# A gated-DeltaNet layer with memory attention: the memory's key products in another PSUM bank, their weights' splits listed 400 instructions earlier

## The chip, the cores and the metric

The kernel runs on one core of a Trainium2 chip. The metric is the device time of one execution in microseconds, as the median of several runs. A profiled execution gives the trace: a record of nearly every instruction on TensorE (PE, with its weight loads as PEld), VectorE (DVE), ScalarE (ACT), GpSimd (POOL) and SyncE (SP), and of the DMA transfers.

## The reference

One decoder layer over 2048 tokens of width 1024: eight heads of a gated delta rule (chunks of 64, head size 128) and four heads of cross-attention to a memory of 256 rows share one input projection and one output projection; then comes a squared-ReLU MLP, with a layer norm after each of the two.

```python
def gdn_mixer(x, mem_k, mem_v, w_in, ...):
    proj = x @ w_in                      # q, k, v, z of 8 heads, gates a, b, and mq of 4 memory heads
    qkv = silu(causal_depthwise_conv(qkv, conv_w))
    ...
    o = chunk_gated_delta_rule(l2_normalize(q), l2_normalize(k), v, g, beta)   # a state per head, chunk after chunk
    ...
def memory_attention(mq, mem_k, mem_v):
    s = einsum('bthd,bmhd->bhtm', q, mem_k) * MEM_HEAD_DIM ** -0.5
    p = softmax(s)
    return einsum('bhtm,bmhd->bthd', p, mem_v)
def sqrelu_mlp(x, w1, w2):
    return square(relu(x @ w1)) @ w2
```

The memory is normalised, and `mem_k` and `mem_v` are its products with `w_mem_k` and `w_mem_v`. They depend on no token, so the kernel makes them once, in its first block. `mem_k` is what the change is about: for each of four memory heads a product of 128 x 1024 by 1024 x 256.

## The kernel before, in words

**Stages.** The 2048 tokens are four blocks of 512. Two super-steps each take two blocks through `mixer` and then run the output projection (`out_seven`, accumulators `ao`) and the MLP (`ff1`, `ff2`, accumulators `fA`, `fB`, `fC`, `f2A` and so on). In `mixer` the eight heads are pipelined: while `dense` and `gate` project head t, `gdn_a` builds the decay matrices of head t-1 and `invert` inverts them, and `gdn_b` carries the state of head t-2 through four chunks of 128. In block 0 the memory's work is spread over the same steps: `memory_rows` first (it makes `mT`, the transposed memory), `memory_keys` for heads 0 and 1 in the next step, for 2 and 3 in the one after it, and then `memory_values`.

**Precision.** A float32 matrix is split into a high part, which ACT casts, and a low part, which DVE makes by a subtraction. `mm3` multiplies with three matmuls: high by high, high by low, low by high. Weights arrive by SP's DMA in `wraw` (three buffers) and are split into `whl` (four buffers): one cast and one subtraction of 128x1024 for a column of weights.

**Names.** `aq`, `ak`, `av`, `az` are the projections of a head, 24 matmuls of 128x512 each; `cq`, `ck`, `cv`, `cz` are what follows from them on ACT and DVE (`cz<-th,az` is the last reader of `az`). `amk` is a key product of the memory, 24 matmuls of 128x256, and `mst` its split, which is stored to `mscr`. `Lq`, `Lc`, `Bc`, `Xc`, `Z32`, `ZT`, `pq`, `pp`, `inv`, `Y` belong to the inverse of a head: `Bc` and `Xc` are a chain of small DVE instructions, `pq` and `pp` the small matmuls after it. `pkq` are products of keys and queries, `ptk`, `ptq`, `ptv` transposes; `vb` is made of `ptv`, `jk` and `kd` of `ptk`, on ACT. The state recurrence of `gdn_b` runs, for each chunk, `pc<-state,ck` and `po<-state,qd` on PE, `R` on DVE, `pc<-R,Y` on PE, `vt` on ACT, `pc<-vt,kd` and `po<-vt,at` on PE, and `state` on DVE.

**PSUM.** Banks are given out by tag: `PBUFS = {"acc": 3, "ga0": 1, "ga1": 1, "pb": 2, "m": 1}`. The projections take `acc`; the memory attention (from the sixth step of the heads on) takes the single bank `m`, which the gates and half of the memory's transposes have had before it.

**Order.** Nothing is issued as the code is run. A recorder notes each instruction with its number and a priority (`o.prio = o.i + self.shift`), and `issue` then replays all of them from line 402, for which reason every row of the profile has the line L402. It is a planner: with modelled durations it picks for each engine, of the instructions whose inputs and buffers are there, the one of the smallest priority. Buffers of a tag are promised in the order in which their first users were noted. Each engine then executes what stands in its list strictly in that order, so a row that waits holds up all that stand behind it.

Of the kernel before, what the change touches and what calls it, by code (L numbers as in the profile page):

```python
# [418 lines left out]
def hybrid_layer(  # L419
# [43 lines left out]
    def slot(name, tag="s0", dt=F32, shape=(P, TB)):  # L463
        return rec.buf(sp, shape, dt, tag, BUFS[tag], name)
# [4 lines left out]
    def bank(name, tag):  # L469
        return rec.buf(ps, (P, TB), F32, tag, PBUFS[tag], name)  # L470
# [32 lines left out]
    rec = Recorder(nc, tc)  # L503
# [25 lines left out]
    def split(src, hi, lo, eng=None):  # L529
        nc.scalar.copy(out=hi, in_=src)  # L530
        (eng or nc.vector).tensor_tensor(out=lo, in0=src, in1=hi.bitcast(F32), op=ALU.subtract)
# [6 lines left out]
    def hilo(src, eng=None):  # L538
        t, hi, lo = pair()
        split(src, hi, lo, eng)  # L540
        return t, hi, lo

    def as_cols(hi, lo):
        hi, lo = hi.rearrange("p (k f) -> p k f", k=KT), lo.rearrange("p (k f) -> p k f", k=KT)
        return [hi[:, k].part(k) for k in range(KT)], [lo[:, k].part(100 + k) for k in range(KT)]

    def mm3(o, lh, ll, rh, rl, start, stop, **kw):
        nc.tensor.matmul(o, lh, rh, start=start, stop=False, **kw)
        nc.tensor.matmul(o, lh, rl, start=False, stop=False, **kw)
        nc.tensor.matmul(o, ll, rh, start=False, stop=stop, **kw)  # L550

    def load_cols(w, u, eng=None):

        rt = rec.buf(wp, (P, 1024), F32, "wraw", NR, "wraw")
        nc.sync.dma_start(out=rt, in_=w[u])
        return as_cols(*hilo(rt, eng)[1:])
# [87 lines left out]
    def memory(step):  # L644
        if step == 0:
            memory_rows()
        elif step < 3:
            for h in (0, 1) if step == 1 else (2, 3):
                memory_keys(h)
        elif step == 3:  # L650
            memory_values()
# [17 lines left out]
            mx.append(t)  # L669

    def memory_keys(h):
        w = load_cols(w_mem_k, h)
        a = bank("amk", "acc")
        for k in range(KT):
            mm3(a[:, :M], w[0][k], w[1][k], mx[k // 2][:, 0, k % 2], mx[k // 2][:, 1, k % 2], k == 0, k == KT - 1)
        st = slot("mst", "th", F32R)
        split(a[:, :M], st[:, :M], st[:, M:])
        nc.sync.dma_start(out=mscr[h, :, :2 * M], in_=st.bitcast(F32))
# [1150 lines left out]
```

## Time and profile before

| | |
|---|---|
| median of three runs | 2760.96 us (2760.94 to 2762.19) |
| the profiled execution's own time | 2760.71 us |
| its span in the trace | 2759.0 us |
| mean granted TensorE clock | 0.997 |
| PE busy | 2719.8 us, 99% of the span, 13589 matmuls |
| DVE, ACT, POOL busy | 2112.2, 1642.3, 403.7 us |

The 1.7 us between the span and the execution's time lie around the program. In a row of the timeline stand the start, the width and the engine, then what is written and what is read, the shapes, and the number of instructions that follow one another without a gap; in brackets, how long the engine had been idle before it and whose end it had waited for. In a row of the windows stand the stretch and its length, then the busy time of PE, PEld, DVE, ACT and POOL with the number of instructions of each, the granted clock, and the share and the rate of the DMA. Where rows overlap a little, an engine has taken up the next instruction before the last one had left it; the cost of one instruction in a row of many is then the distance between two starts.

### The profile page before, as it was taken

To read this page: it belongs to the slowest core of one execution; us is meant where nothing else is said; L and a number is where in the kernel's file an instruction comes from. 1 tells how busy PE (TensorE), PEld (TensorE's weight loads), DVE (VectorE), ACT (ScalarE), POOL (GpSimd) and SP (SyncE) were. 2 spreads that over 40 slices of the span, in tenths; PEclk is the share of its full clock that TensorE was granted. 3 is DMA by queue.
4 is the path that set the end of the run, shared out by engine and by line. 5 is a ranking of instruction groups with operands and counts; after the bars stand their busy time and mean duration, and the time that the engine had idled before them with its cause. 6 is when DMAs were issued, how large, how long until landed. Compare 5 with 4: busy or idle time off the path is not lost.

```text
span 2759.0 us, 42405 instructions
## 1 busy us (share of the span) xinstructions
PE 2719.8 (99%) x13589; PEld 2267.0 (82%) x13589; DVE 2112.2 (77%) x5652; ACT 1642.3 (60%) x4082; POOL 403.7 (15%) x1030
## 2 busy tenths in 40 slices
PE   9999999999999999999999999999999999999998
PEld 7888888887788888888888888888887788888887
DVE  7889889998777777665778887888978665657575
ACT  7678767676485556334446676677855655544342
POOL 3233223321000000000023321223201000000000
PEclk9999999999999999999999999999999999999999
DMA  8565558876788888766754344444578744477673
GB/s 327 207 234 205 215 182 288 290 258 228 269 284 302 280 285 297 268 211 205 265 209 149 138 155 174 169 147 159 206 251 280 249 145 152 163 252 243 205 239 116
DMA packets 208543, 613.99 MB, mean 223 GB/s; under 512 B 23072, under 2 KB 32192, under 8 KB 188352
## 3 DMA queue, kind: packets, MB, share of 16 engines
q1 hardware_dynamic: 207888, 611.23, 63.5%
q8 instruction: 107, 1.75, 0.2%
q14 instruction: 116, 0.95, 0.1%
q10 hardware_dynamic: 432, 0.05, 0.0%
HBM read 436.54 MB, written 174.65 MB: 222 GB/s over the span
## 4 chain that ended last, share of the span: by engine, by line
PE 88%; ACT 7%; DVE 4%; issue 1%; POOL 1%; DMA 0%; DVEq 0%; SPq 0%; POOLq 0%; ACTq 0%
PE f2A L402 13%; PE fA L402 12%; PE ao L402 8%; PE f2C L402 6%; PE fC L402 6%; PE az L402 5%; PE aq L402 5%; PE av L402 5%; PE ak L402 5%; PE f2B L402 3%; PE fB L402 3%; PE amq L402 3%; PE pc L402 3%; PE po L402 2%; PE pkq L402 1%
## 5 line engine op out<-in xcount | busy, mean ns | idle before, releaser
L402 DVE TENSOR_TENSOR whl<-wraw,whl 128x512 fp32r<-128x512 f32 (+2 forms) x294 | 257.2, 884 | 109.4 <-ACT whl L402 107.0
L402 ACT CAST whl<-wraw 128x512 fp32r<-128x512 f32 (+2 forms) x294 | 226.5, 780 | 158.0 <-PE fC L402 52.0
L402 PE MATMUL fA<-B,whl 128*128 128x512 f32 x1152 | 277.2, 389 | 1.8 <-ACT B L402 1.5
L402 ACT CAST X<-X 128x1024 fp32r<-128x1024 f32 x118 | 123.9, 1052 | 236.2 <-DMA X<-xsc 196.2
L402 PE MATMUL f2A<-whl,X 128*128 128x512 f32 x1152 | 262.1, 389 | 0.0
L402 PEld LDWEIGHTS fA<-B,whl 128*128 128x128 f32 x1152 | 216.1, 188 | 47.5 <-ACT B L402 1.9
L402 PEld LDWEIGHTS f2A<-whl,X 128*128 128x128 f32 x1152 | 216.2, 188 | 44.9
L402 DVE TENSOR_TENSOR X<-X,X 128x1024 fp32r<-128x1024 f32 x118 | 144.2, 1223 | 129.0 <-ACT X L402 128.8
L402 PE MATMUL aq<-T,whl 128*128 128x512 f32 x768 | 214.3, 408 | 10.0 <-ACT T L402 5.5
L402 PE MATMUL az<-T,whl 128*128 128x512 f32 x768 | 213.0, 406 | 0.0
L402 PE MATMUL ak<-T,whl 128*128 128x512 f32 x768 | 211.4, 406 | 0.0
L402 PE MATMUL av<-T,whl 128*128 128x512 f32 x768 | 210.4, 404 | 0.0
L402 PE MATMUL fC<-B,whl 128*128 128x512 f32 x768 | 185.4, 389 | 0.3 <-DVE B L402 0.3
L402 PE MATMUL f2C<-whl,X 128*128 128x512 f32 x768 | 174.7, 389 | 0.0
L402 PEld LDWEIGHTS fC<-B,whl 128*128 128x128 f32 x768 | 144.1, 188 | 30.7 <-DVE B L402 0.8
L402 PEld LDWEIGHTS f2C<-whl,X 128*128 128x128 f32 x768 | 144.1, 188 | 29.9
L402 PEld LDWEIGHTS aq<-T,whl 128*128 128x128 f32 x768 | 136.5, 191 | 32.7 <-ACT T L402 5.5
L402 POOL TENSOR_SCALAR ve<-mv 128x1 f32<-128x1 f32 x34 | 16.4, 483 | 962.0 <-DVE mv L402 961.5
L402 PEld LDWEIGHTS av<-T,whl 128*128 128x128 f32 x768 | 137.3, 189 | 22.7
L402 PEld LDWEIGHTS ak<-T,whl 128*128 128x128 f32 x768 | 136.4, 189 | 23.5
L402 PEld LDWEIGHTS az<-T,whl 128*128 128x128 f32 x768 | 135.9, 189 | 21.6
L402 PE MATMUL ao<-whl,X 128*128 128x512 f32 x528 | 140.1, 404 | 3.5 <-DVE whl L402 1.3
(287 smaller groups left out, 6300.8 us busy)
## 6 DMA issues: line engine op xcount, KB each, us to landing
whl<-wsc SPq DMA_DIRECT2D x108, 1024.0 KB, 4.8
wraw<-in_w_ff_dram SPq DMA_DIRECT2D x106, 512.0 KB, 4.5
X<-xsc SPq DMA_DIRECT2D x96, 512.0 KB, 3.9
wsc<-whl SPq DMA_DIRECT2D x36, 1024.0 KB, 5.2
whl<-tsc SPq DMA_DIRECT2D x64, 512.0 KB, 4.7
xsc<-hB SPq DMA_DIRECT2D x96, 256.0 KB, 3.4
xo<-cat SPq DMA_DIRECT2D x80, 256.0 KB, 3.9
wraw<-in_w_in_dram SPq DMA_DIRECT2D x35, 512.0 KB, 5.9
```

Source lines behind the costliest of these rows:

```text
L402: o.fn(*[res(a) for a in o.args], **{k: res(v) for k, v in o.kw.items()})
```

## The change

The weights of a key product are now noted with priorities 400 smaller (the DMA, the cast and the subtraction), and the product takes the bank `m` in place of one of the three `acc`.

```diff
     def memory_keys(h):
+        rec.shift = -400
         w = load_cols(w_mem_k, h)
-        a = bank("amk", "acc")
+        rec.shift = 0
+        a = bank("amk", "m")
         for k in range(KT):
             mm3(a[:, :M], w[0][k], w[1][k], mx[k // 2][:, 0, k % 2], mx[k // 2][:, 1, k % 2], k == 0, k == KT - 1)
```

Since the planner starts from other priorities and other banks, the lists of all engines change, from the first key product on until the output projection of the first super-step; from there on they are the same again, instruction by instruction. Three places matter here.

PE, second head of block 0, at the first two key products; a piece of the difference. `az` is the gate's projection of the first head and `aq` the query projection of the second; `T_...` are the tokens.

```order
 L402 MATMUL az<-T_221,whl 128x512
-L402 MATMUL amk<-mT,whl 128x256 x4
+L402 MATMUL amk<-mT,whl 128x256 x24
 L402 MATMUL aq<-T_160,whl 128x512
 L402 MATMUL aq<-T_165,whl 128x512
-L402 MATMUL amk<-mT,whl 128x256 x44
 L402 MATMUL aq<-T_160,whl 128x512 x2
 L402 MATMUL aq<-T_165,whl 128x512
...
 L402 MATMUL aq<-T_226,whl 128x512
 L402 MATMUL aq<-T_221,whl 128x512 x2
+L402 MATMUL amk<-mT,whl 128x256 x24
 L402 MATMUL aq<-T_226,whl 128x512
```

Before, two key products (4 and 44 matmuls) stand around the first two matmuls of `aq`. Now one stands whole ahead of `aq`, and the other behind its twentieth matmul.

DVE, the same place, with the buffers' numbers. Before, the low halves of the two key weights (`whl_995`, `whl_1029`) and of `aq`'s weight (`whl_1056`, made of `wraw_862`) stand in one group behind `cz`:

```order
L402 SCALAR_TENSOR_TENSOR cz_1101<-th_1080,az_999 128x512
L402 STREAM_SHUFFLE Bc_114<-Xc_106 128x32
L402 STREAM_SHUFFLE Bc_116<-Xc_108 128x12
L402 TENSOR_TENSOR whl_995<-wraw_757,whl_995 128x1024
L402 TENSOR_TENSOR Bc_114<-Bc_114,Lc_962 128x32
L402 TENSOR_TENSOR Bc_116<-Bc_116,Lc_1060 128x12
L402 TENSOR_TENSOR whl_1029<-wraw_818,whl_1029 128x1024
L402 TENSOR_TENSOR Xc_106<-Xc_106,Bc_114 128x32
L402 TENSOR_TENSOR Xc_108<-Xc_108,Bc_116 128x12
L402 TENSOR_TENSOR whl_1056<-wraw_862,whl_1056 128x1024
```

Now the key weights' low halves stand some 50 rows earlier, and `aq`'s, again made of `wraw_862`, stands between the steps of the convolutions:

```order
L402 SCALAR_TENSOR_TENSOR ck_1010<-raw_704,cw_96,ck_1010 128x512
L402 TENSOR_TENSOR Bc_114<-Bc_114,Lc_970 128x20
L402 TENSOR_TENSOR Bc_116<-Bc_116,Lc_1061 128x4
L402 SCALAR_TENSOR_TENSOR cv_1024<-raw_918,cw_96,cv_1024 128x512
L402 TENSOR_TENSOR Xc_106<-Xc_106,Bc_114 128x20
L402 TENSOR_TENSOR Xc_108<-Xc_108,Bc_116 128x4
L402 TENSOR_TENSOR whl_1057<-wraw_862,whl_1057 128x1024
L402 STREAM_SHUFFLE Bc_114<-Xc_106 128x24
```

Compared with before, 21 rows that stood ahead of `aq`'s low half now stand behind it, `cz` among them: six of 128x512 (`ck<-th`, two of `cv<-raw`, `kq<-ck`, `cv<-th`, `cz`) and 15 small ones of the inverse.

PE, the state recurrence of the first head of block 0, while the second head's inverse runs. Before, pieces of the fourth key product stand between its steps:

```order
L402 MATMUL pc<-vt,kd 128x128
L402 MATMUL po<-vt,at 128x128
L402 MATMUL pq<-ZT_1503,inv 128x32 x2
L402 MATMUL amk<-mT,whl 128x256 x2
L402 MATMUL pc<-state,ck 128x128
L402 MATMUL po<-state,qd 128x128
L402 MATMUL amk<-mT,whl 128x256 x5
L402 MATMUL pc<-R,Y 128x128
L402 MATMUL pp<-inv 112x32 x2
L402 MATMUL amk<-mT,whl 128x256 x3
```

Now the third key product stands ahead of this place and the fourth behind it, and the recurrence stands with small matmuls and transposes alone:

```order
L402 MATMUL ptv_1559<-ident_75,cv_440 128x128 x4
L402 MATMUL pc_752<-R_1570,Y_154 128x128
L402 MATMUL ptk_1576<-ident_75,ck_1010 128x128 x4
L402 MATMUL pc_752<-vt_1583,kd_536 128x128
L402 MATMUL po_891<-vt_1583,at_864 128x128
L402 MATMUL pp_1593<-inv_143,inv_133 112x32 x2
L402 MATMUL pc_1600<-state_102,ck_367 128x128
L402 MATMUL po_891<-state_102,qd_855 128x128
L402 MATMUL pc_1600<-R_1607,Y_154 128x128
L402 MATMUL pq_1619<-Lq_1040,inv_136 128x32 x2
L402 MATMUL pc_1600<-vt_1621,kd_536 128x128
L402 MATMUL po_891<-vt_1621,at_864 128x128
```

The ten matmuls of `amk` between the links are gone from this place.

On SP the raw loads of the key weights move ahead too: the first two past one store of a split weight, the third and fourth past the raw loads of the next head's projections.

## The prediction

> **What bounds the kernel now.** The page's first part and its chain come first:
>
> ```profile
> PE 2719.8 (99%) x13589; PEld 2267.0 (82%) x13589; DVE 2112.2 (77%) x5652; ACT 1642.3 (60%) x4082; POOL 403.7 (15%) x1030
> PE 88%; ACT 7%; DVE 4%; issue 1%; POOL 1%; DMA 0%; DVEq 0%; SPq 0%; POOLq 0%; ACTq 0%
> ```
>
> PE is busy all the time. No matmul is taken away or added, so the change can only give or take PE's idle time and stretches of lower clock. The windows by stage show where those are (length, busy time of PE, PEld, DVE, ACT and POOL, clock, DMA):
>
> ```profile
> 75.00:105.00 30.00, 25.51 (x130) 21.72 (x130) 27.02 (x136) 14.77 (x27) 1.83 (x6) 0.89 0.53 199
> 105.00:135.00 30.00, 30.00 (x206) 27.34 (x205) 27.35 (x85) 25.09 (x87) 12.44 (x29) 1.00 0.64 214
> 600.00:740.00 140.00, 130.50 (x685) 107.57 (x684) 116.50 (x340) 85.38 (x237) 19.73 (x48) 0.98 0.72 248
> 740.00:1400.00 660.00, 659.14 (x2940) 543.23 (x2939) 466.22 (x687) 332.92 (x491) 16.72 (x32) 1.00 0.76 260
> ```
>
> The key products lie in the first two rows, from 81.5 us on. The first has 4.5 us of idle PE and a clock of 0.89; the second has no idle at all. The third is the end of the mixer, with 9.5 us idle. From there on the lists of all engines are the same before and after, so the fourth row and what follows can change only in when it starts. The timeline of PE, in the first of these stretches:
>
> ```profile
> 81.52 0.63 PE L402 MATMUL amk<-mT,whl 128*128 128x256 f32 x4
> 86.60 1.19 PE L402 MATMUL aq<-T,whl 128*128 128x512 f32 x2 [4.45 <-DVE Bc L402]
> 87.84 7.06 PE L402 MATMUL amk<-mT,whl 128*128 128x256 f32 x44
> 94.73 5.18 PE L402 MATMUL aq<-T,whl 128*128 128x512 f32 x22
> 99.75 0.62 PE L402 MATMUL ak<-T,whl 128*128 128x512 f32 x2
> ```
>
> PE stops for 4.45 us ahead of `aq`. The bracket names `Bc`, which `aq` does not read. DVE's timeline tells which of its rows it was:
>
> ```profile
> 83.38 0.75 DVE L402 SCALAR_TENSOR_TENSOR cv<-raw,cw,cv 128x512 f32<-128x512 f32 x1
> 84.15 0.17 DVE L402 STREAM_SHUFFLE Bc<-Xc 128x8 f32<-128x8 f32 x1
> 84.22 0.69 DVE L402 TENSOR_TENSOR kq<-ck,kq 128x512 fp32r<-128x512 f32 x1
> 84.82 0.26 DVE L402 TENSOR_TENSOR Bc<-Bc,Lc 128x28 f32<-128x28 f32 x2
> 85.77 0.69 DVE L402 SCALAR_TENSOR_TENSOR cz<-th,az 128x512 f32<-128x512 f32 x1
> 86.56 1.22 DVE L402 TENSOR_TENSOR whl<-wraw,whl 128x1024 fp32r<-128x1024 f32 x1
> 89.19 1.23 DVE L402 TENSOR_TENSOR whl<-wraw,whl 128x1024 fp32r<-128x1024 f32 x1
> 90.33 0.02 DVE L402 LOAD_MASK_SELECT Bc<-Xc  x1
> ```
>
> `cz` ends at 85.77 + 0.69 = 86.46 and `aq` starts 0.14 later: `cz` is the last reader of `az`, two of the three `acc` banks are held by the two key products, and `aq` takes the bank that `az` leaves. The key product itself had stopped after four matmuls for its weight's low half, which DVE made from 86.56 to 87.78; it goes on at 87.84. In windows of 3.41 us, on whose edges the clock changes:
>
> ```profile
> 81.07:84.48 3.41, 1.08 (x7) 0.80 (x5) 3.41 (x16) 2.54 (x5) 0.43 (x2) 1.00 0.00 0
> 84.48:87.89 3.41, 1.24 (x3) 0.56 (x3) 3.41 (x15) 0.37 (x1) 0.47 (x1) 0.50 0.00 0
> 87.89:91.30 3.41, 3.41 (x16) 3.41 (x17) 3.41 (x17) 0.00 (x0) 0.00 (x0) 0.50 0.61 185
> ```
>
> After a window with 1.08 us of work PE got half its clock for 6.83 us.
>
> **The stall that goes.** From 81.52 to 99.75 PE does 48 matmuls of `amk` and 24 of `aq`. At full clock:
>
> ```profile
> 126.73 1.55 PE L402 MATMUL amk<-mT,whl 128*128 128x256 f32 x11
> 128.12 0.39 PE L402 MATMUL pc<-vt,kd 128*128 128x128 f32 x2
> ```
>
> One of `amk` is (128.12 - 126.73)/11 = 0.126 us; one of `aq`, by the rows above, (99.75 - 94.73)/22 = 0.228. The work is 48 x 0.126 + 24 x 0.228 = 11.5 us, and it took 18.2: **6.7 us** lost. With the key product in `m`, `aq` has a free `acc` bank; with the weight split some 50 rows sooner, the first product has its low half. Both causes go, hence -6.7.
>
> **What is late next there.** First, `aq`'s own low half. Its subtraction ended where the 90.33 row starts. 21 rows move behind it: from start to start 0.67 for each of two `cv<-raw` (83.38 to 84.05, the shuffle ahead of 84.15), 0.60 for each of four others like `kq` (84.22 to 84.82), and 15 small ones of about 0.09 (0.07 between 84.15 and 84.22): 5.1 us. So it ends near 85.3. PE comes to it after 24 key matmuls and two of `aq`, at 81.5 + 3.1 + 0.45 = 85.05: 0.3 us of waiting. Second, there is one bank `m`: the second product waits until the first is split into `mst`.
>
> ```profile
> L402 DVE TENSOR_TENSOR mst<-amk,mst x3: 417/424/424, 92.7 to 129.8; 128x256 fp32r<-128x256 f32 x3
> ```
>
> In the new list 17 rows stand between `aq`'s low half and this subtraction (five wide, 3.1 us, and twelve small, 1.1), so it ends at 85.3 + 4.2 + 0.4 = 89.9; PE gets there 20 `aq` later, at 84.9 + 4.6 = 89.5. That is 0.4 (0 if DVE is a little earlier, 1 if later). Together **+0.7**.
>
> **What loses its cover.** In the 105:135 row PE has no idle, because pieces of the fourth key product stand between the links of the first head's state recurrence. They are gone from there. The links' lengths are read where the recurrence runs bare, at the end of the mixer:
>
> ```profile
> 691.41 0.60 PE L402 MATMUL ptv<-ident,cv 128*128 128x128 f32 x4
> 691.77 2.09 PE L402 MATMUL ao<-whl,X 128*128 128x512 f32 x8
> 692.05 1.14 ACT L402 ACTIVATE vb<-ptv,vbs 128x128 f32<-128x128 f32 x4 [1.06 <-PE ptv L402]
> 692.46 0.35 DVE L402 SCALAR_TENSOR_TENSOR R<-pc,nbe,vb 128x128 f32<-128x128 f32 x1
> 701.49 0.38 PE L402 MATMUL pc<-vt,kd 128*128 128x128 f32 x2
> 701.71 0.39 PE L402 MATMUL po<-vt,at 128*128 128x128 f32 x2
> 702.32 0.49 PE L402 MATMUL pc<-state,ck 128*128 128x128 f32 x2 [0.22 <-DVE state L402]
> 703.25 0.49 PE L402 MATMUL pc<-R,Y 128*128 128x128 f32 x2 [0.22 <-DVE R L402]
> 704.15 0.49 PE L402 MATMUL pc<-vt,kd 128*128 128x128 f32 x2 [0.41 <-ACT vt L402]
> 109.07 0.53 PE L402 MATMUL pq<-Lq,inv 128*128 128x32 f32 x4
> 109.43 0.94 PE L402 MATMUL av<-T,whl 128*128 128x512 f32 x3
> ```
>
> From `pc<-vt` to `pc<-state` it is 0.83 us, to `pc<-R` 0.93, to the next `pc<-vt` 0.90; from `ptv` to a `pc<-R` that needs `vb`, 692.46 + 0.35 + 0.06 - 691.41 = 1.46. PE has between them, in the new list: `ptv` 0.36; `pc`, `ptk` 0.22 + 0.36; `pc`, `po`, `pp` 0.22 + 0.22 + 0.36; `pc`, `po` 0.44; `pc`, `pq` 0.58; `pc`, `po` 0.44; then `pc`, `po`, `pp`, `ptq`, which fill their link. (A pair of `pc` is 701.71 - 701.49; four transposes, and the four rows of `pq`, 0.36 to the next row.) Gaps: 1.10 + 0.32 + 0.03 + 0.49 + 0.32 + 0.39 = 2.65. ACT adds to them: its new list has four `vb` and four copies of the inverse ahead of one `vt`, and seven `jk` and `kd` and three copies ahead of the next; at 1.14/4 = 0.28 each the second group lasts some 2.8 us where two links and a half last 2.3. That is up to 1.2 in both, so 2.6 to 3.9. The lower bound is 0.1: before, the same links with other work around them showed no idle, and the second head's projections could be ready elsewhere. I take **+3.3**, nearer to the bare rows, since it is their order that the new list has.
>
> **The clock there.** Idle of 3.3 us within about 7 leaves windows of some 1.5 to 2.2 us of work. The nearest rows:
>
> ```profile
> 702.29:705.70 3.41, 1.91 (x10) 1.34 (x10) 1.33 (x3) 1.84 (x6) 0.00 (x0) 1.00 0.50 156
> 630.61:634.02 3.41, 2.16 (x14) 1.77 (x15) 2.69 (x12) 3.41 (x11) 1.06 (x2) 1.00 0.57 223
> 707.49 2.50 PE L402 MATMUL ao<-whl,xh 128*128 128x512 f32 x5 [2.64 <-ACT whl L402]
> ```
>
> Half clock followed the first of these and not the second. If it comes, 6.83 us at half clock double about 2.5 us of work that is not hidden in the links: +2.5. I leave it out of the forecast, since more of the window estimates lie above 1.91 than below, and keep it as a case. The Trainium skill, "TensorE: Matmul & The Clock Gate", section "Why this matters for your kernels", asks for no PE gaps of over about 3 us and says that a window of idle brings the half clock back. By that rule the bare stretch, with gaps of 1.1 us and little more, keeps its clock, and 2758.0 would hold without this case. This trace is harsher than the rule: half clock began at 705.70, 0.84 us into an idle of 2.64 that had followed only short gaps.
>
> **The rest at no cost.** SP's loads of the key weights move past a store and past raw loads:
>
> ```profile
> wraw<-in_w_in_dram SPq DMA_DIRECT2D x35, 512.0 KB, 5.9
> ```
>
> A load lands 5.9 us after its issue, and the projections use it a head (96 matmuls of 0.228, 22 us) later; were a weight late, PE would lose up to these 5.9. The ACT casts move with DVE's subtractions; ACT is 60% busy. At the end of the mixer (idle until 707.49) the new list has the same three short links, so I count nothing, with 1 us either way.
>
> **The sum.** -6.7 + 0.7 + 3.3 = -2.7, against the profiled execution's 2760.71: **2758.0**. The median of before lies 0.25 above that execution, far below the 0.2%, 5.5 us, which is about what a measurement of this kernel can tell from no change. Faster therefore means below 2755.4, slower above 2766.5.
>
> **The rivals.**
>
> *Half clock in the bare stretch.* -2.7 + 2.5 = -0.2: 2760.5. For it speaks the 702.29 row, against it the 630.61 row.
>
> *The stall stays in part.* `aq`'s low half comes 4 to 5 us later than summed, because DVE waits for ACT's casts as before: the saving shrinks to about 2, and the bare stretch costs 3.3 + 0.7: about +2, 2762.7. Against it: DVE was full from 81.07 to 91.30, so that its rows had their inputs.
>
> *Faster.* The recurrence finds its links shorter, as in 105:135 (up to 1.7 us lost, say 1.2), and the end of the mixer, which starts 5 us sooner while its DMA does not wait for it, shrinks its wait of 2.64 by 0.5 to 2.6, say 1.6: -6.7 + 0.7 + 1.2 - 1.6 = -6.4: 2754.3. For it: no idle in 105:135. Against it: the fillers there were the very matmuls that moved.
>
> *Slower: one bank `m`.* If the subtraction into `mst` ends later than about 91.8, that is 2 us after the sum above, PE stands idle for more than 2.3 us ahead of the second product, as it did from 82.15 (86.60 - 4.45) to the clock's fall at 84.48. Then a wait of 3.0 and half clock (6.83/2 = 3.4) come back, in other clothes, and the bare stretch falls on its worst end, 3.9 + 2.5: -6.7 + 6.4 + 6.4 = +6.1: 2766.8. For it: a single buffer, with a reader at the end of DVE's full list. Against it: the sum has it late by 0.4 only.
>
> **The numbers.** The forecast 0.32, half clock in the stretch 0.17, the stall in part 0.05: these three are within 0.2%, 0.54. Faster 0.26, slower 0.20. The likeliest case alone spans 2754.8 to 2760 (3.3 moved between 0.1 and 3.9, and 1 us for the rest). The range reaches into both outer cases: 2753.0 to 2767.0.
>
> **What would show it.** Right: no idle over 0.6 us between 81 and 95 us, `aq` going on behind the first key product, the clock at 1.00 there; then, from about 115 us, brackets of 0.3 to 1.1 us ahead of `pc<-R`, `pc<-vt`, `pc<-state`, summing to 3.3. Wrong: a wait of `amk` for `mst` or of `aq` for `whl` of over 1 us, half clock near 120 us, or a wait ahead of 707 us that has changed by over 1 us.

## The result, and the profile after

| | before | after |
|---|---|---|
| median of ten runs, taken together | 2761.64 us (2759.99 to 2764.28) | 2767.26 us (2763.19 to 2770.64) |
| ratio, 95% interval | | 1.0020 [1.0012, 1.0028] |
| span of the profiled execution | 2759.0 us | 2765.8 us |

The changed kernel is slower by 5.6 us, just outside the range that was given (to 2767.0), and slower where the forecast of -2.7 had it faster. The page after, its span and its busy times:

```profile
span 2765.8 us, 42393 instructions
PE 2725.9 (99%) x13589; PEld 2268.9 (82%) x13589; DVE 2114.4 (76%) x5652; ACT 1639.2 (59%) x4082; POOL 407.8 (15%) x1030
```

The matmuls are as many as before. PE is "busy" 6 us longer with them, since the record of a matmul at half clock or behind a wait is longer. The windows by stage, of after:

```profile
75.00:105.00 30.00, 30.00 (x161) 25.78 (x159) 29.61 (x119) 18.19 (x33) 2.38 (x7) 1.00 0.67 243
105.00:135.00 30.00, 27.59 (x175) 23.53 (x173) 22.14 (x100) 20.65 (x74) 7.14 (x21) 1.00 0.55 210
600.00:740.00 140.00, 129.82 (x658) 106.69 (x658) 114.89 (x329) 81.55 (x221) 17.84 (x41) 0.95 0.69 242
740.00:1400.00 660.00, 658.08 (x2931) 541.72 (x2930) 462.20 (x682) 333.35 (x493) 14.20 (x30) 1.00 0.76 260
```

The first row has lost its idle and its half clock. The second has gained 2.4 us of idle, and the third a lower clock (0.95 for 0.98). At the first place, PE's timeline and then two rows of DVE's:

```profile
82.16 3.04 PE L402 MATMUL amk<-mT,whl 128*128 128x256 f32 x24
85.04 5.21 PE L402 MATMUL aq<-T,whl 128*128 128x512 f32 x22
90.08 3.04 PE L402 MATMUL amk<-mT,whl 128*128 128x256 f32 x24
92.96 0.63 PE L402 MATMUL aq<-T,whl 128*128 128x512 f32 x2
```

```profile
84.05 1.21 DVE L402 TENSOR_TENSOR whl<-wraw,whl 128x1024 fp32r<-128x1024 f32 x1
89.38 0.41 DVE L402 TENSOR_TENSOR mst<-amk,mst 128x256 fp32r<-128x256 f32 x1
```

There is no idle in it. `aq`'s low half is there at 85.26, and the split that frees bank `m` ends at 89.79, ahead of the second product at 90.08. At the second place, the bare recurrence:

```profile
122.94 0.49 PE L402 MATMUL pc<-R,Y 128*128 128x128 f32 x2 [1.15 <-DVE R L402]
124.25 0.49 PE L402 MATMUL pc<-vt,kd 128*128 128x128 f32 x2 [0.26 <-ACT vt L402]
124.58 0.39 PE L402 MATMUL po<-vt,at 128*128 128x128 f32 x2
126.11 0.49 PE L402 MATMUL pc<-R,Y 128*128 128x128 f32 x2 [0.22 <-DVE R L402]
126.81 0.60 PE L402 MATMUL pq<-Lq,inv 128*128 128x32 f32 x4 [0.20 <-ACT Lq L402]
128.19 0.49 PE L402 MATMUL pc<-state,ck 128*128 128x128 f32 x2 [0.24 <-DVE state L402]
```

And the waits behind it that the account below rests on, from 327 us on:

```profile
328.11 0.66 PE L402 MATMUL ptv<-ident,cv 128*128 128x128 f32 x4 [0.69 <-ACT Y L402]
329.62 1.11 PE L402 MATMUL aab<-T,abw 128*32 128x512 f32 x4 [0.38 <-DVE T L402]
635.42 0.50 PE L402 MATMUL ao<-whl,X 128*128 128x512 f32 x1 [1.14 <-ACT whl L402]
638.74 6.59 PE L402 MATMUL ao<-whl,X 128*128 128x512 f32 x16 [2.82 <-ACT X L402]
735.96 1.52 PE L402 MATMUL ao<-whl,X 128*128 128x512 f32 x4 [1.84 <-DVE whl L402]
818.82 0.50 PE L402 MATMUL fA<-B,whl 128*128 128x512 f32 x1 [1.49 <-ACT B L402]
2168.16 0.49 PE L402 MATMUL fA<-B,whl 128*128 128x512 f32 x1 [1.49 <-ACT B L402]
```

Since the lists differ, the traces are compared by work: each matmul gets the median distance to the next start that its kind has in the trace of before; these are added up, and the times at which the same sum is reached are compared. That is how far each run lags (+) or leads (-) at some points in the time of before. It is exact where both lists have the same matmuls behind them, and good to about 1 us inside a shuffled stretch.

| profile of | 100 | 118 | 137 | 220 | 320 | 350 | 790 | 870 | 2700 |
|---|---|---|---|---|---|---|---|---|---|
| after | -6.3 | -6.7 | -2.7 | -1.8 | -1.8 | +0.3 | +3.1 | +5.4 | +6.8 |
| e1, new head, old tail | -7.0 | -7.4 | -3.3 | -1.6 | -1.6 | -1.6 | -1.9 | -1.9 | -2.1 |
| e2, old head, new tail | +0.4 | +0.5 | +0.5 | +0.6 | +0.7 | +2.8 | +3.8 | +5.7 | +7.2 |
| e3, weights ahead only | -7.2 | -7.6 | +6.9 | +5.7 | +6.6 | +7.0 | +8.8 | +14.3 | +14.1 |
| e4, bank only | +0.6 | +1.0 | +1.8 | +1.8 | +2.6 | +2.5 | +4.9 | +5.0 | +5.0 |
| e9, two heads, old tail | -6.6 | -7.0 | +2.9 | +2.6 | +2.5 | +2.5 | +2.4 | +2.7 | +2.7 |
| e11, two heads, own tail | -7.4 | -7.8 | +3.1 | +3.0 | +3.3 | +3.3 | +9.0 | +9.3 | +10.9 |

The profile of after starts 0.7 late, before anything differs. Less these, it gains 7.4 us by 118 us, gives back 4.9 of them by 220, and stands at -2.5: nearly the forecast of -2.7. Then it loses 8.6 us in a part of the program that has no key product at all. (The table compares single executions. The profiled one of before, 2760.71, lies 0.9 below its median, and those of e3 and e11 lie 2.4 and 2.7 above theirs, so its totals are not the differences of the medians.)

### The profile page after: what moved, and what is told of

Read it like the earlier page. It is cut to its first block, busy times and chain, and to the rows that moved or that the text cites. A ratio compares the mean times of both kernels' runs of the same rounds, so it can differ in the third digit from the quotient of the medians.

```text
span 2765.8 us, 42393 instructions
## 1 busy us (share of the span) xinstructions
PE 2725.9 (99%) x13589; PEld 2268.9 (82%) x13589; DVE 2114.4 (76%) x5652; ACT 1639.2 (59%) x4082; POOL 407.8 (15%) x1030
## 4 chain that ended last, share of the span: by engine, by line
PE 84%; ACT 7%; DVE 5%; DMA 2%; issue 1%; POOL 1%; DVEq 0%; SPq 0%; ACTq 0%; POOLq 0%
PE f2A L402 13%; PE fA L402 12%; PE ao L402 7%; PE f2C L402 6%; PE fC L402 6%; PE aq L402 5%; PE az L402 5%; PE av L402 5%; PE ak L402 4%; PE f2B L402 3%; PE fB L402 3%; PE pc L402 3%; PE amq L402 2%; PE po L402 2%; PE pkq L402 1%
```

## The experiments

Theory A: the change's own places do what was forecast, and the loss comes from the lists of later heads, of the output projection and of the first MLP products, which the planner shuffled along. Theory B: the loss is made at the key products and only seen later. To tell them apart, the planner was run twice in one kernel, with the old and with the new priorities and bank, and the lists were grafted at a time of its own modelled clock, in nanoseconds; that time is called CUT below:

```diff
+        before, after = self.plan(0, "acc"), self.plan(-400, "m")
+        one, two = after, before
+        head = [o for o, t in one if t < 165000.0]
+        done = set(o.i for o in head)
+        out = head + [o for o, t in two if o.i not in done]
```

**e1** is this with CUT at the planner's 165 us. 

> The lists of the changed kernel as far as the planner's 165 us (all key products lie ahead of that), and behind them the lists of the kernel before. Theory A (the change's own places give the 2.8 us that were forecast; the loss comes from the lists of the later heads and of the first output projection, which the planner shuffled and which were counted at nothing): about 2759, faster than before by some 2.8 us, and the waits of the kernel before at 630, 705 and 732 us are back. Theory B (the loss is made at the key products and is only seen later, as loads or buffers that come late): about 2767, as the changed kernel.

Measured: 2759.68 us against 2762.12, ratio 0.9994 [0.9985, 1.0003]. Theory A's size, though the interval reaches to no change. The wait of before is back at its own size:

```profile
630.04 0.66 PE L428 MATMUL pmT<-ident,pr 128*128 128x128 f32 x4 [1.71 <-DVE pm L428]
```

**e2** has `before` and `after` changed about in these lines. 

> The other way round: the lists of the kernel before as far as the planner's 165 us, with its banks and its stall of 4.45 us, then the lists of the changed kernel. Theory A: slower than before by the tail alone, the measured +5.6 and the 2.8 that the head no longer gives: about +8, 2770. Theory B: about 2762, as before.

Measured: 2768.95, ratio 1.0025 [1.0015, 1.0035], 6.8 us slower where some 8 were expected: theory A. The new tail brings its waits with it, though its head is the old one:

```profile
637.71 0.50 PE L428 MATMUL ao<-whl,X 128*128 128x512 f32 x1 [1.14 <-ACT whl L428]
641.03 4.14 PE L428 MATMUL ao<-whl,X 128*128 128x512 f32 x10 [2.83 <-ACT X L428]
```

The two parts add up: -2.4 and +6.8 make +4.4, and the whole change measured +5.6.

**e3** leaves the bank as it was:

```diff
-        a = bank("amk", "m")
+        a = bank("amk", "acc")
```

> Only the priorities 400 smaller; the key products keep an acc bank. The list of PE has 48 key matmuls in one piece ahead of aq. Forecast's reading: the weights' low halves are there, 48 x 0.126 = 6.0 us of work cover the time until cz frees the bank at about 86.5, so the stall of 6.7 us goes, and the fourth product still stands between the links of the first recurrence: -5 to -6.5 by 320 us. Rival reading (the bank was the cause): aq waits for cz as before, 2 us or more idle stay ahead of it. Theory A for the end: the tail's lists are others again, so the total may be off from that by some 5 us either way; theory B: the total is what the head gives.

Measured: 2772.33, ratio 1.0038 [1.0026, 1.0051]. The stall at 82 us goes, as forecast, and without the bank. But the lead of 7.2 us is a lag of 6.9 at 137, and of 6.6 at 320 where a lead of 5 to 6.5 was expected: PE now stands in front of the first head's inverse. PE's rows and the two clock windows:

```profile
87.08 5.63 PE L402 MATMUL aq<-T,whl 128*128 128x512 f32 x24
114.56 0.84 PE L402 MATMUL pp<-inv 128*128 128x32 f32 x4 [1.39 <-DVE inv L402]
118.26 1.08 PE L402 MATMUL pq<-YP,inv 128*128 128x64 f32 x4 [2.86 <-DVE YP L402]
```

```profile
111.38:114.79 3.41, 2.02 (x19) 1.94 (x18) 2.99 (x12) 2.86 (x9) 1.83 (x4) 1.00 0.95 305
114.79:118.20 3.41, 0.61 (x4) 0.47 (x3) 3.20 (x12) 0.87 (x4) 0.53 (x3) 0.50 0.97 380
```

Half clock lasts 20.5 us from there. In the list of the whole change, 24 matmuls of the next head's `aq` fill that place; thirteen of them, in its timeline:

```profile
115.21 3.24 PE L402 MATMUL aq<-T,whl 128*128 128x512 f32 x13
```

**e4** leaves the priorities as they were and changes the bank alone (`rec.shift = 0`). 

> Only the bank m; the weights' splits keep their priorities. The list of PE has 2 key matmuls, two of aq, 22 key matmuls, some of aq, then 24 key matmuls. Forecast's reading: the bank wait of 4.45 us goes but the first product still waits for its weight's low half: 2 to 4 us idle stay at 82 to 88 us, and since the later products keep standing between the recurrence's links, there is no bare stretch: -1 to -4 by 320 us. Rival reading (the bank alone was the cause): no idle there. Theory A: the total again off by some 5 us either way through the tail; theory B: the total is what the head gives.

Measured: 2765.64, ratio 1.0012 [1.0003, 1.0021]. The stall does not shrink at all, and where -1 to -4 by 320 us was expected the trace has +2.6:

```profile
87.92 4.64 PE L402 MATMUL amk<-mT,whl 128*128 128x256 f32 x22 [5.35 <-DVE whl L402]
```

The first product waits there for its low half. So of the two causes that the prediction named, the late split alone holds PE for the whole time; the bank comes on top.

**e5** is e1 with CUT at 100 us, and `acc` banks for the third and fourth product. 

> The lists of the changed kernel only as far as the planner's 100 us (the first two key products, in bank m, with their weights split ahead), then the lists of the kernel before, in which the third and fourth product (in acc banks) stand between the links of the first recurrence. If the forecast's two terms are right apart (stall gone -6.7, bare stretch about +4.5 as the first graft's trace has it), this has the first without the second: -6 or a little more, about 2756, faster by 0.2%, with no idle of over 0.5 us between 81 and 135 us. If the stall's gain is only moved work that is paid back later anyway, it is at about -2, like the first graft.

Measured: 2765.32 against 2762.59, ratio 1.0008 [0.9999, 1.0018]: a miss of the expected 2756, and no answer to its question, because PE waits at the seam for the first head's inverse, which DVE has not reached:

```profile
106.26 1.03 PE L430 MATMUL pq<-ZT,inv 128*128 128x32 f32 x4 [3.91 <-DVE Xp L430]
```

**e6, e7, e8** are e1 with the cut later, to see which part of the new tail costs what.

> New lists to the planner's 420 us, old ones behind. The tail as several separate places: adds the place at 327 to 345 us to the first graft (-2.4): about 0, 2762. The tail as one place (the start of the output projection at 635): still -2.4.

> New lists to the planner's 680 us: adds the start of the output projection, where the new lists wait 1.1 and 2.8 us and lose half a window of clock: separate places, about +2.5 to +3, 2765; one place: about +4 to +5, 2767.

> New lists to the planner's 770 us, old ones in the first products of the MLP: all but the wait of 1.49 us at 818 us. Separate places: +3 to +5, 2765 to 2767, and no wait at 818; one place: as the run before it.

Measured: 2761.39, 2762.94 and 2762.53 us against 2762.59; ratios 0.9999 [0.9990, 1.0008], 1.0000 [0.9991, 1.0009], 1.0001 [0.9992, 1.0010]. By medians that is -1.2, +0.4 and -0.1, after e1's -2.4. Each step is within its interval, so that timing does not place the loss ahead of 770 us. e7 missed both readings, which expected +2.5 or more, and e8 the +3 to +5 of separate places. The traces do place some of it. By the working of the table, e6, e7 and e8 each lose 2.1 us from 220 to 350, as after does; from 622 to 665 e7 and e8 lose 2.2 and e6, with the old list there, nothing. The waits at 327 and 635 us stand in the runs whose lists have them, at the sizes shown for after, and e8 has 0.35 us at 818 in place of 1.49. What remains by medians between e8 and the whole change, some 5 us, lies behind 770 us.

**e10** asks for that part alone: the old lists to 770 us, the new ones behind. 

> Old lists to the planner's 770 us, new ones behind: the first products of the MLP alone, where the new lists wait 1.49 us at 818. Separate places: +1.5 to +2.5, 2764 to 2765, the wait of 1.49 there, sometimes with 1.7 us for half a window of clock. One place (the loss sits in the start of the output projection): 0.

Measured: 2765.65 against 2761.66, ratio 1.0011 [1.0003, 1.0020]: +4.0, more than the +1.5 to +2.5 of the reading by separate places, and clear of the 0 of the other, with the wait:

```profile
817.91 0.49 PE L428 MATMUL fA<-B,whl 128*128 128x512 f32 x1 [1.49 <-ACT B L428]
```

In its trace the lag grows by 2.5 us from 790 to 870, and by 1.6 at 2165, of which more below.

**e9** makes the edit for the first two products alone, with the old tail from 165 us:

```diff
-        rec.shift = -400
+        rec.shift = -400 if h < 2 else 0
-        a = bank("amk", "m")
+        a = bank("amk", "m" if h < 2 else "acc")
```

> The edit for the first two key products alone (their splits 400 ahead, bank m); the third and fourth keep their priorities and an acc bank; the lists behind the planner's 165 us are those of the kernel before. The planner now puts 24 matmuls of the fourth product between the links of the first recurrence. If the single bank m is what uncovered the recurrence (the fourth product waits there until the third is split): the stall's -6.7 stays and the bare stretch's +4.5 shrinks to 1 or less: -5 to -6.5, about 2756.5. If the recurrence is bare for another reason (the inverse comes later because aq's split stands ahead of it): about -2, like the first graft.

Measured: 2763.70, ratio 1.0006 [0.9997, 1.0015]; a miss for both readings. The recurrence is filled, as intended (third row below), but the gap has moved ahead of it, to the inverse:

```profile
114.80 0.60 PE L428 MATMUL pp<-inv 128*128 128x32 f32 x4 [0.89 <-POOL inv L428]
118.07 1.08 PE L428 MATMUL pq<-YP,inv 128*128 128x64 f32 x4 [2.67 <-DVE YP L428]
126.68 1.12 PE L428 MATMUL amk<-mT,whl 128*128 128x256 f32 x6
```

with 10.2 us of half clock from 116.8 on. In after, e3, e5 and e9 alike, what PE meets once the stall is gone is the first head's chain, inverse and then recurrence, on DVE and ACT; after has it covered in the inverse, e9 in the recurrence, and neither in both. And the chain itself comes later. Its first transpose on DVE, in before and then in after:

```profile
103.46 0.30 DVE L402 STREAM_TRANSPOSE ZT<-Z 128x128 f32<-128x128 f32 x1
```

```profile
108.12 0.30 DVE L402 STREAM_TRANSPOSE ZT<-Z 128x128 f32<-128x128 f32 x1
```

With the bank alone (e4) it stays at 103.12; with the smaller priorities it is at 107.24 (e3), 107.47 (e1) and 107.90 (e9), though PE is 7 us ahead. In the list of after, 13 more rows stand ahead of it on DVE, among them three weight splits and six steps of `cq` and `ck`. That is the second reading of this run in kind, an inverse that comes later, though not its -2. How much of the time is lost to the later chain, and how much to PE's reaching it sooner, no run separates.

**e11** is e9's edit with the planner's own lists to the end. 

> The same edit for the first two heads, without the graft: the planner's own lists to the end. To 165 us as e9: -5 to -6.5. Its tail differs from that of the kernel before up to about 740 us and is the same in the MLP: a tail of its own, +-4, so 2752 to 2761; if the tails shuffled by such an edit are always worse, +2 or more over e9.

Measured: 2768.87, ratio 1.0026 [1.0017, 1.0036], 5.2 us over e9 with the same head: outside the 2752 to 2761, and as the last clause had it, another shuffled tail that is worse.

**e12** was meant to beat both kernels: e1 with the cut at 300 us. 

> A version meant to beat both: the new lists to the planner's 300 us, that is up to the end of the first block, then the old ones. It keeps the first graft's gain, has its seam where fewer instructions differ, and ends ahead of the place at 327 us that costs 2 us. If the loss sits in separate places of the tail: -2.5 to -3.5, 2758.5 to 2759.5, and from the seam on the waits of the kernel before, at their sizes. If a later seam brings the loss along: about 0, as the version with the seam at 420.

Measured: 2765.49 against 2761.50, ratio 1.0014 [1.0005, 1.0023]: it does not, and both readings missed. It leads by 2.6 us at 306, and loses 5.2 at the seam, with half clock behind it:

```profile
311.23 0.49 PE L428 MATMUL pc<-vt,kd 128*128 128x128 f32 x2 [0.65 <-ACT vt L428]
313.57 1.24 PE L428 MATMUL pkq<-kq 128*128 128x256 f32 x6 [1.63 <-DVE Bc L428]
```

So e1 is the fastest version measured, and its 2.4 us are not clear of no change.

## Why the prediction was wrong

**The stall that goes, -6.7: right.** It gained 7.0 to 7.4. The two causes were not equal, though: e4 shows that the bank alone gives nothing, e3 that the split alone suffices for this place.

**Late next, +0.7: too high.** Neither `aq` nor the second product waited.

**The lost cover, +3.3: right in kind, low in size.** 4.0 us by 137 and 4.9 by 220, over the upper bound of 3.9. The brackets shown add up to 2.1 us, and two more at 131.88 and 135.34 to 0.7. Part of the rest is not idle by the records: short matmuls behind a wait come slower, `po` 0.33 us after its `pc` (124.25 to 124.58) where the sum had 0.22. What is left was not traced further. The forecast priced this from the bare links alone; that DVE comes to the inverse 4.7 us later it did not see. The clock stayed full, as the forecast had it. All of the head: -2.5 against -2.7, but that closeness is luck in part: the gain was larger than -6.7 + 0.7 by 1.4, and the lost cover larger than 3.3 by 1.6.

**"From there on the lists of all engines are the same", and "at the end of the mixer ... I count nothing, with 1 us either way": the step that failed.** It was wrong twice. PE's lists meet again only at 853 us of before (858.5 of after), inside the MLP, not at the output projection, as the part on the change and the forecast had it; those of ACT, DVE and SP differ here and there until 1038 to 1072 us of before. So the wait at 818 lay in a stretch that was taken for unchanged. And behind the key products the forecast priced the shuffled lists by the short links of the recurrence alone, at nothing. The waits of after that have no like in before are of other kinds: `ptv` and `aab` at 327, the casts of `whl` and `X` ahead of the output projection's first products at 635, `B` ahead of `fA` at 818. By the trace of after: 2.1 us from 320 to 350, 3.2 from 622 to 665, 2.3 from 790 to 870, and 1.6 at 2165, where the lists are the same. (In e2, e7 and e8 the second of these is 2.1 to 2.2: half clock lasts 3.41 us there, and 6.83 in after.) By timing the new tail alone costs 6.8, where the forecast had nothing, with 1 us either way.

**The rivals.** The rival that had the kernel slower, by a wait for the single bank `m`, is not what happened: no such wait is in the trace. That its 2766.8 is near the measured time is chance. The faster rival had a part: the wait ahead of `ao<-whl,xh` did shrink, by 0.8 us, and half clock behind it lasted 3.41 us in place of 6.83. `ao` gave that back at 736, and not by a longer wait: before waits as long there, in two pieces,

```profile
732.82 0.50 PE L402 MATMUL ao<-whl,X 128*128 128x512 f32 x1 [1.12 <-DVE y L402]
733.95 15.69 PE L402 MATMUL ao<-whl,X 128*128 128x512 f32 x68 [0.64 <-DVE whl L402]
```

but half clock, 3.41 us from 736.6 on, followed in after and not in before.

Why should a shuffled tail be slower, not faster? The planner's costs know nothing of the clock, and a list is measured only after it is planned. Of the four tails that the planner made after some edit of the head (after, e3, e4, e11), all four lost from 220 us to the end: 8.6, 8.4, 3.2 and 7.9 us by the table, 1.6 of it in after and e11 at 2165, where the lists are the same. That the old list was picked among several by its time would explain it, but no run shows that.

## What to carry to other kernels

Where a planner sets the order, cost an edit on the whole list up to the row where both lists meet, and find that row first; a reshuffled rest is a cost of its own, here 3 to 9 us by the traces, and larger than the 2.4 us that the edit gained in e1. Grafting one kernel's list onto the other's, with the cut at a few places, separates an edit from its reshuffle, but a seam can make waits of its own. And before a hole on the busiest engine is counted as a gain, look at which chain comes next, and whether the edit moves that chain too: here the first head's inverse and recurrence took back two thirds of the 7.4 us.

## What the runs showed of the hardware

The clock goes by windows, not by single gaps. In the fourteen profiles (both kernels and e1 to e12), PE's work in each window of 3.413 us, up to 2690 us, can be held against the clock of the next. Of the windows at full clock with less than 1.8 us of work, 36 of 37 were followed by half clock; of those with 1.8 to 2.4 us, 8 of 42; of the others, some 10,800, none. Three such windows, two of after and one of before:

```profile
634.18:637.59 3.41, 0.60 (x2) 0.19 (x1) 3.41 (x10) 3.41 (x5) 0.00 (x0) 1.00 0.93 312
2166.78:2170.19 3.41, 1.75 (x6) 1.23 (x7) 3.41 (x7) 3.41 (x8) 0.00 (x0) 1.00 0.96 356
```

```profile
2159.78:2163.19 3.41, 1.92 (x9) 1.24 (x7) 3.41 (x7) 2.86 (x6) 0.00 (x0) 1.00 0.90 312
```

The last two hold the same wait of the same list:

```profile
2162.93 0.49 PE L402 MATMUL fA<-B,whl 128*128 128x512 f32 x1 [1.49 <-ACT B L402]
```

1.49 us of idle in both, but in after the next gap, of 0.27 us, falls into the same window, and in before it lies beyond the window's edge. That costs 1.6 us. The windows' edges lie elsewhere in the program in each run (0.2 us into a multiple of 3.413 in e7, 2.6 in before), and this wait was followed by half clock in 7 of the fourteen profiles, whatever their lists. So whether this place costs 1.6 us differs from run to run with where the edges fall. It may be part of why ten runs of one kernel spread over 4 to 7 us: the mean clock of the ten runs of after was 0.994 to 0.997, and 0.994 or 0.995 in the three that took over 2770 us. No trace of those shows which windows it was.

The Trainium skill, "TensorE: Matmul & The Clock Gate", section "What's actually happening", has the window as free-running, 3413 ns long; the edges agree. Its section "Why this matters for your kernels" warns of gaps of over about 3 us; here a gap of 1.49 us was enough, together with one of 0.27 us in the same window.
